# Five probability row buffers, held-back score products and a third transpose bank in a hybrid decoder trunk

## The chip, the cores and the metric

The kernel runs on one core of a Trainium2 chip. The metric is device time in microseconds of one execution; the profile's span is the time from the first to the last instruction of the program.

## The reference

The trunk has two layers over 1040 tokens (16 learned meta tokens in front of 1024) of width 1024, all in float32. Each layer is a pre-RMSNorm, a mixer, a multiplication by SiLU of a gate, an output projection and a residual addition. Layer 0 is multi-head latent attention with 8 heads; layer 1 is a gated linear recurrence (RG-LRU). A final RMSNorm follows.

```python
proj = h @ w_in                              # 384 | 256 | 64 | 1024
q_lat, kv_lat, k_rope, gate = jnp.split(proj, ...)
q  = rmsnorm(q_lat, q_norm_g) @ w_uq         # 8 heads x (128 + 64)
kv = rmsnorm(kv_lat, kv_norm_g) @ w_ukv      # 8 heads x (128 + 128)
...
s = (q_nope . k_nope + q_rope . k_rope) * scale
p = softmax(where(causal mask, s, -1e30))
attn = p @ v
y = attn * silu(gate);  h = h + y @ w_out
```

## The kernel before, in words

Every product is made of three single-pass products on the high and low parts of its operands (`mm3`). `hi_of` makes the high part on ACT (a copy with rounding), `lo_of` the low part on DVE (the difference). Nearly every tile therefore goes PSUM to ACT to DVE before TensorE can use it again.

PSUM has eight banks. The ring of a tag is its number of buffers: before attention, tag `t` (transposes, `ps_t`) has 2 and tag `m` (products, `ps_m`) has 6. In attention `t` has 2, `g` (projections and weighted sums) has 2, and `s2` (scores) has 2 buffers of two banks each.

*Start and latent stage.* The token tiles are taken in the order 8, 0, 1, ..., 7; tile 8 has 16 rows and is multiplied in a packed form (`mm_stack`). `x_tile` normalises a tile on ACT and DVE, transposes it on TensorE (`transpose_in`) and splits it. `lat_mm` makes the products `pq` and `pk` of a tile in two banks of `ps_m`; `lat_norm` normalises them, `lat_post` transposes them (`qt`, `kt`) and splits them. The row `g_a` is spread over all partitions with a product (`rb_ga`) and copied back by DVE. The stage of the rotary queries and gates (`rope_q_chunk`, `a_gate`) follows.

*Attention.* The 1040 rows are cut into 9 tiles of 116 rows (the last has 112). A unit is one head and one tile t; it uses the keys up to its own end, so its row is 116 (t + 1) columns long. `scores` makes the products in `s2` banks (the last tile's row needs both buffers), adds the mask and takes the extreme on DVE (line 501), writes exponentials to a row buffer `p` on ACT (line 509) and normalises the row (DVE for t < 6, ACT behind that). `transposes` turns the row in groups of three key blocks (`tr` = 0, 1, 2), each in one bank `pt`, and splits each into `pth` and `ptl`. `weighted` multiplies three tiles at a time with the values. The main loop runs over the 72 units:

```python
    for u, (h, t) in enumerate(units):
        if u + LEAD < len(units):
            scores(*units[u + LEAD])
        ...
        for f in fill[h, t]:
            f()
        transposes(h, t)
```

`fill` holds the K, Q and V projections of later chunks and heads (`k_unit`, `q_unit`, `v_unit`), and `LEAD` is 3. The row buffers `p` are three, each of 1040 columns.

*What sets the order.* The program text is not the issue order. A planner simulates the engines and puts on each one, among the instructions whose inputs and buffers it thinks ready, the one that was written first. On the chip each engine then keeps this order. `behind(marks, f, ...)` adds an order: what `f` issues on the engine of a mark comes behind that mark on that engine; it is an order of issue, with no wait for the mark's end.

Of the kernel before, what the change touches and what calls it, by code (L numbers as in the profile page):

```python
# [17 lines left out]
P = 128  # L18
# [26 lines left out]
GRP = 3  # L45
CH = [(g * GRP * QB, min(GRP * QB, T - g * GRP * QB)) for g in range((NQB + GRP - 1) // GRP)]
CHW = GRP * QB
MASKW = 8 * QB


def segments(e):
# [11 lines left out]
def trunk(ctx, tc, x, meta, a_norm_g, a_w_in, a_q_g, a_kv_g, a_w_uq, a_w_ukv, a_w_out,  # L63
# [12 lines left out]
    def bc(t):  # L76
        return t.bitcast(F32)

    def hi_of(dst, src):
        nc.scalar.activation(dst, src, AF.Copy)  # L80

    def lo_of(dst, src, hi):
        nc.vector.tensor_tensor(dst, src, bc(hi), ALU.subtract)  # L83

    def mm3(ps, lh, ll, rh, rl, start, stop, **kw):
        nc.tensor.matmul(ps, lh, rh, start=start, stop=False, **kw)  # L86
        nc.tensor.matmul(ps, lh, rl, start=False, stop=False, **kw)  # L87
        nc.tensor.matmul(ps, ll, rh, start=False, stop=stop, **kw)  # L88

    def mm_stack(ps, xp, k, n, wh, wl):  # L90
        if k:
# [16 lines left out]
    def ps_tag(tag, bufs):  # L108
        return lambda name: ps_pool[0].tile([P, 512], F32, name=name, tag=tag, bufs=bufs)

    ps_t, ps_g, ps_m = ps_tag("t", 2), ps_tag("g", 2), ps_tag("m", 6)
    def ps_2(name):
        return ps_pool[0].tile([P, 2, 512], F32, name=name, tag="s2", bufs=2)

# [11 lines left out]
    make_identity(nc, ident)  # L126

    def rms_r(ms, n, w, name):
        v = sml.tile([P, w], F32, name=f"v_{name}", tag="rv")[:n]
        r = sml.tile([P, w], F32, name=f"r_{name}", tag="rr")[:n]  # L130
        t = sml.tile([P, w], F32, name=f"t_{name}", tag="rt")[:n]
        root = nc.scalar.activation(t, ms, AF.Sqrt, bias=eps[:n])
        nc.vector.tensor_scalar(v, ms, -0.5, -0.5 * EPS, ALU.mult, ALU.add)
        nc.vector.reciprocal(t, t)
        if w == 1:
            nc.vector.scalar_tensor_tensor(r, t, v, t, ALU.mult, ALU.mult)
        else:
            nc.vector.tensor_tensor(r, t, t, ALU.mult)
            nc.vector.tensor_tensor(r, r, v, ALU.mult)
        nc.vector.scalar_tensor_tensor(r, r, 1.5, t, ALU.add, ALU.mult)  # L140
        return r, root
# [16 lines left out]
    def transpose_in(xn, n, t0, xth, xtl, name):  # L158
        for j in range(2):
            pt = ps_t(f"xt_{name}_{j}")  # L160
            pv = pt.rearrange("p (a b) -> p a b", b=P)[:, :, :n]
            for a in range(4):
                k = 4 * j + a
                nc.tensor.transpose(pv[:, a], xn[:n, k * P:(k + 1) * P], ident[:n, :n])
            hs = xth[:, 4 * j:4 * j + 4, t0:t0 + n]
            hi_of(hs, pv)
            lo_of(xtl[:, 4 * j:4 * j + 4, t0:t0 + n], pv, hs)

    def load_wcols(w, c0, nk, ncols, name):
        st = stage(name)  # L170
# [51 lines left out]
    def x_tile(i, xs):  # L222
        t0, n = TOK[i]
        j0 = t0 if n == P else 0
        junk = xth[:, :, j0:j0 + P]
        marks = normalise(xs[:n], xs[:n], n, g_a, junk, f"a{i}")
        if n < P:
            nc.gpsimd.memset(bc(xpk[:, :, n:STK]), 0.0)
            transpose_in(xs, n, 0, xpk, xpk[:, :, STK:], f"a{i}")
            nc.gpsimd.tensor_copy(xth[:, :, t0:t0 + n], bc(xpk[:, :, :n]))  # L230
            nc.gpsimd.tensor_copy(xtl[:, :, t0:t0 + n], bc(xpk[:, :, STK:]))
        else:
            transpose_in(xs, n, t0, xth, xtl, f"a{i}")
        return marks
# [26 lines left out]

    def lat_norm(i, pq, pk):
        t0, n = TOK[i]
        ms = sml.tile([P, 2], F32, name=f"lms{i}", tag="lms")[:n]
        lt = pa1.tile([P, QL + KVL], F32, name=f"lt{i}", tag="lt", bufs=2)[:n]
        nc.scalar.activation(lt[:, :QL], pq[:n, :QL], AF.Square, scale=float(QL ** -0.5), accum_out=ms[:, 0:1])
        nc.scalar.activation(lt[:, QL:], pk[:n, :KVL], AF.Square, scale=float(KVL ** -0.5), accum_out=ms[:, 1:2])
        kc = pa1.tile([P, 2, HR], F32, name=f"kc{i}", tag="kc", bufs=2)[:n]
        kn = pa1.tile([P, 2, HR], F32, name=f"kn{i}", tag="kn", bufs=2)[:n]
        kr = pa1.tile([P, 3, DR], F32R, name=f"kr{i}", tag="kr", bufs=1)[:n]  # L270
        krv = pk[:n, KVL:KVL + DR].rearrange("p (a b) -> p a b", a=2)
        nc.vector.tensor_tensor(kc, krv, csk[:n, i:i + 1, :HR].broadcast_to([n, 2, HR]), ALU.mult)
        nc.vector.tensor_tensor(kn, krv, csk[:n, i:i + 1, HR:].broadcast_to([n, 2, HR]), ALU.mult)
        r, _ = rms_r(ms, n, 2, f"lat{i}")
        nc.vector.scalar_tensor_tensor(lt[:, :QL], pq[:n, :QL], r[:, 0:1], g_q[:n, :QL], ALU.mult, ALU.mult)
        nc.vector.scalar_tensor_tensor(lt[:, QL:], pk[:n, :KVL], r[:, 1:2], g_q[:n, QL:], ALU.mult, ALU.mult)
        nc.vector.tensor_tensor(kc[:, 0], kc[:, 0], kn[:, 1], ALU.subtract)
        nc.vector.tensor_tensor(kc[:, 1], kn[:, 0], kc[:, 1], ALU.add)
        kf = kc.rearrange("p a b -> p (a b)")
        nc.vector.tensor_copy(kr[:, 0], kf)  # L280
        nc.vector.tensor_tensor(kr[:, 1], kf, bc(kr[:, 0]), ALU.subtract)
        nc.vector.tensor_copy(kr[:, 2], bc(kr[:, 0]))
        return lt, bc(kr.rearrange("p a b -> p (a b)"))
# [28 lines left out]
    n0 = TOK[order[0]][1]  # L312
    nc.sync.dma_start(g_a[:n0, :], a_norm_g[0:1, :].broadcast_to([n0, D]))
    xs0 = x_load(order[0])
    marks = x_tile(order[0], xs0)
    rbs = []
    for c in range(0, D, 512):
        ps = ps_m(f"rb_ga{c}")
        nc.tensor.matmul(ps, ones, g_a[0:1, c:c + 512], start=True, stop=True)
        rbs.append(ps)  # L320
    for c in range(0, D, 512):
        nc.vector.tensor_copy(g_a[:, c:c + 512], rbs[c // 512])
    for k in range(2):
        behind(marks, load_wlat, k)
    x_tile(order[1], x_load(order[1]))
    for k in range(2, KT):
        behind(marks, load_wlat, k)
    x_tile(order[2], x_load(order[2]))
# [60 lines left out]
    def a_gate(m):  # L389
        raw = load_wcols(a_w_in, LATW + m * P, KT, P, f"wg{m}")  # L390
        wh, wl = split_page(raw, [P, KT, P], f"wg{m}")
        for c, (c0, cw) in enumerate(CH):
            ps = ps_m(f"ga{m}_{c}")[:, :cw]
            for k in range(KT):
                mm3(ps, wh[:, k], wl[:, k], xth[:, k, c0:c0 + cw], xtl[:, k, c0:c0 + cw], k == 0, k == KT - 1)
            nc.scalar.activation(Y[:, m, c0:c0 + cw], ps, AF.Silu)

    for m in range(KT):
        a_gate(m)
        if m < 6:  # L400
            if m % 3 == 0:
                wr = rope_w(m // 3)
            rope_q_chunk(m // 3, m % 3, *wr)
# [2 lines left out]


    st_p1.close()
    st_p3, ps_pool[0] = open_pool("ps3", space=PSUM)
    st_at, pat = open_pool("at", bufs=2)  # L410
    maskt = pat.tile([QB, MASKW], F32, name="maskt", bufs=1)
# [1 line left out]
    nc.gpsimd.affine_select(out=maskt[:, MASKW - QB:], in_=maskt[:, MASKW - QB:], pattern=[[-1, QB]],  # L413
                            compare_op=ALU.is_ge, fill=-NEG, base=0, channel_multiplier=1)
    KV, QW, KK, QQ, VV, PP, PT = {}, {}, {}, {}, {}, {}, {}

    def load_pair(h):
        st = stage(f"wkv{h}")
# [9 lines left out]
    def k_unit(h, c):  # L428
# [4 lines left out]
        c0, cw = CH[c]  # L433
        ps = ps_g(f"pk{h}_{c}")[:, :cw]
        for k in range(VKT):
            mm3(ps, kvw[0][:, k, hh * 256:hh * 256 + DN], kvw[1][:, k, hh * 256:hh * 256 + DN],
                klh[:, k, c0:c0 + cw], kll[:, k, c0:c0 + cw], k == 0, k == VKT - 1)
        kh, kl = KK[h]
        hi_of(kh[:, c0:c0 + cw], ps)
        lo_of(kl[:, c0:c0 + cw], ps, kh[:, c0:c0 + cw])  # L440

    def q_unit(h, c):
        qw, hh = QW[h // 2], h % 2
# [27 lines left out]
    def scores(h, t):  # L471
# [7 lines left out]
        tiles = [segs[i:i + 2] for i in range(0, len(segs), 2)]  # L479
        m = sml.tile([QB, 2], F32, name=f"m{h}_{t}", tag="m")[:n]  # L480
        l = sml.tile([QB, 2], F32, name=f"l{h}_{t}", tag="l")[:n]
        p = pat.tile([QB, T], F32, name=f"p{h}_{t}", tag="p", bufs=3)[:n]
        pss = []
        a, b_, r_ = qh[:, off:off + n], ql[:, off:off + n], qr[:, off:off + n]
        for s, sg in enumerate(tiles):
# [10 lines left out]
            ns, k0 = len(sg), sg[0][0]  # L496
            pv = ps2[:n, :ns, :w]
            if s == len(tiles) - 1:
                lo = MASKW - QB - (ns * w - n)
                mk = maskt[:n, lo:lo + ns * w].rearrange("p (a b) -> p a b", a=ns)  # L500
                MKD[h, t] = nc.vector.tensor_tensor_reduce(pv, pv, mk, 1.0, -NEG, ALU.add, ALU.min, m[:, s:s + 1])  # L501
            else:
                nc.vector.tensor_reduce(m[:, s:s + 1], pv, AX.XY, ALU.min)
# [16 lines left out]
    def transposes(h, t):  # L520
# [8 lines left out]
        for tr in range(g + 1):  # L529
# [3 lines left out]
            pv = pt[:, :GRP * QB].rearrange("p (a b) -> p a b", b=QB)[:, :, :n]  # L533
            for j, kb in enumerate(kbs):
                k0, nk = QBLK[kb]
                nc.tensor.transpose(pv[:nk, j], p[:, k0:k0 + nk], ident[:n, :n])  # L536
            nfull = sum(1 for kb in kbs if QBLK[kb][1] == QB)
            parts = [(0, nfull, QB)] if nfull else []
            if nfull < len(kbs):
# [1 line left out]
            for j0, j1, nk in parts:  # L541
                dh = pth[:nk, j0:j1, off:off + n]
                hi_of(dh, pv[:nk, j0:j1])
                lo_of(ptl[:nk, j0:j1, off:off + n], pv[:nk, j0:j1], dh)

    def weighted(h, g):
        c0, cw = CH[g]
# [106 lines left out]
    for i, t in enumerate((5, 7, 8)):  # L654
        fill[H - 1, t].append(lambda i=i: a_out0(i, ps_g))
    load_pair(0)
    k_unit(0, 0)
    q_unit(0, 0)
    for u in range(-LEAD - 2, 0):
        for c in (1, 2):  # L660
            if 3 * c - LEAD - 2 == u:
                k_unit(0, c)
            if 3 * c - LEAD - 1 == u:
                q_unit(0, c)
# [2 lines left out]
    pending = None  # L667
    for u in range(LEAD):
        scores(*units[u])
    for u, (h, t) in enumerate(units):  # L670
        if u + LEAD < len(units):
            scores(*units[u + LEAD])
        if pending:
            weighted(*pending)
            pending = None
        for f in fill[h, t]:
            f()
        transposes(h, t)
        if t % 3 == 2:
            pending = (h, t // 3)  # L680
    weighted(*pending)
# [299 lines left out]
    def late(i, c, done):  # L981
        ms = sml.tile([P, 1], F32, name=f"msb{i}", tag="msb", bufs=2)
        square(i, c, ms)
        v = sml.tile([P, 1], F32, name=f"v_f{i}", tag="rv")
        r = sml.tile([P, 1], F32, name=f"r_f{i}", tag="rr")
        t = sml.tile([P, 1], F32, name=f"t_f{i}", tag="rt")
        nc.scalar.activation(t, ms, AF.Sqrt, bias=msa[i])
# [140 lines left out]
```

## Time and profile before

| | before |
|---|---|
| median of 3 runs | 913.55 us (913.08 to 913.59) |
| the profiled execution | 913.81 us |
| its span | 912.0 us |
| TensorE (PE) busy | 887.0 us, 97% |
| VectorE (DVE) busy | 584.5 us, 64% |
| ScalarE (ACT) busy | 469.0 us, 51% |
| GpSimd (POOL) busy | 44.5 us, 5% |

Busy time is the time in which an engine had at least one instruction in work. Successive products overlap, so that a busy PE need not be at its peak; idle time, on the other hand, is time without any product. A view of waits puts the idle time of an engine down to the instruction that ended it.

### The profile page before, as it was taken

How to read it: one execution, taken by the hardware profiler on the slowest of the kernel's cores; microseconds unless marked ns; L12 is line 12 of the kernel's file. 1: busy time of each engine (PE TensorE's matmuls, PEld its weight loads, DVE VectorE, ACT ScalarE, POOL GpSimd, SP SyncE). 2: the span in 40 equal slices, each digit the busy share in tenths (PEclk: the TensorE clock that was granted, in tenths of full speed). 3: DMA queues.
4: the chain of work that ended last, by engine and by line, in shares of the span. 5: the costliest groups of instructions: out<-in, count | busy, mean ns of one | idle time of the engine just before them, and what ended most of it. 6: DMA issues, size and time to landing. Idle time of an engine off the chain costs nothing.

```text
span 912.0 us, 13696 instructions
## 1 busy us (share of the span) xinstructions
PE 887.0 (97%) x5291; PEld 817.2 (90%) x5291; DVE 584.5 (64%) x1211; ACT 469.0 (51%) x941; POOL 44.5 (5%) x46
## 2 busy tenths in 40 slices
PE   7999999999999999999999999999999999999996
PEld 4989999998999999999998878799989989897885
DVE  6567434226676676776677457757393764868997
ACT  6554323215665656646656235634835457365455
POOL 3000000000000000000000000000020110212200
PEclk9999999999999999999999999999999999999999
DMA  7123254321010010010003435241111121237624
GB/s 261 62 59 92 61 135 127 87 72 57 16 56 18 14 58 16 17 63 16 17 24 116 152 99 179 78 81 47 47 47 49 45 57 37 95 91 230 140 69 184
DMA packets 71169, 72.25 MB, mean 79 GB/s; under 512 B 15056, under 2 KB 52688, under 8 KB 71104
## 3 DMA queue, kind: packets, MB, share of 16 engines
q1 hardware_dynamic: 68928, 67.19, 24.0%
q0 software_dynamic: 2176, 4.19, 2.7%
q8 instruction: 41, 0.67, 0.3%
q14 instruction: 24, 0.20, 0.1%
HBM read 58.65 MB, written 12.71 MB: 78 GB/s over the span
## 4 chain that ended last, share of the span: by engine, by line
PE 92%; ACT 3%; DVE 2%; issue 1%; DMA 1%; SPq 0%; ACTq 0%; DVEq 0%
PE pt L536 4%; PE pu L88 3%; PE ga L86 3%; PE pu L86 3%; PE ga L87 3%; PE ga L88 3%; PE pu L87 3%; PE ao L86 3%; PE ao L88 3%; PE ao L87 3%; PE pg L87 3%; PE pg L88 3%; PE pg L86 3%; PE s L491 2%; PE b L86 2%; PE b L88 2%
## 5 line engine op out<-in xcount | busy, mean ns | idle before, releaser
L509 ACT ACTIVATE p<-s,m 116x116 f32<-116x116 f32 (+4 forms) x80 | 55.4, 694 | 42.8 <-PE pt L536 15.2
L80 ACT ACTIVATE pth<-pt 116x348 fp32r<-116x348 f32 (+5 forms) x152 | 57.4, 397 | 28.6 <-PE pt L536 24.9
L83 DVE TENSOR_TENSOR ptl<-pt,pth 116x348 fp32r<-116x348 f32 (+5 forms) x152 | 63.9, 437 | 9.8 <-ACT pth L80 9.2
L88 PE MATMUL pu<-x2h,l_wu 128*128 128x348 f32 (+1 forms) x192 | 61.5, 321 | 0.4 <-DVE l_wu L83 0.4
L86 PE MATMUL ga<-xth,h_wg 128*128 128x348 f32 (+1 forms) x192 | 61.7, 322 | 0.0
L88 PE MATMUL ga<-xth,l_wg 128*128 128x348 f32 (+1 forms) x192 | 61.7, 321 | 0.0
L86 PE MATMUL pu<-x2h,h_wu 128*128 128x348 f32 (+1 forms) x192 | 61.7, 322 | 0.0
L87 PE MATMUL pu<-x2l,h_wu 128*128 128x348 f32 (+1 forms) x192 | 61.7, 321 | 0.0
L87 PE MATMUL ga<-xtl,h_wg 128*128 128x348 f32 (+1 forms) x192 | 61.6, 321 | 0.0
L501 DVE CUSTOM_DVE_ANT_0 s<-s,maskt 116x116 f32<-116x116 f32 (+8 forms) x72 | 49.4, 686 | 17.6 <-PE s L495 17.6
L536 PE MATMUL pt<-ident,p 116*116 116x116 f32 (+1 forms) x360 | 54.2, 262 | 0.9 <-DVE ptl L83 0.4
L87 PE MATMUL pg<-x2l,h_wbg 128*128 128x512 f32 x128 | 50.6, 395 | 0.0
L86 PE MATMUL ao<-wah,yh_a 128*128 128x512 f32 x128 | 50.5, 396 | 0.0
L88 PE MATMUL pg<-x2h,l_wbg 128*128 128x512 f32 x128 | 50.3, 393 | 0.0
L86 PE MATMUL pg<-x2h,h_wbg 128*128 128x512 f32 x128 | 50.2, 392 | 0.0
L88 PE MATMUL ao<-wah,yl_a 128*128 128x512 f32 x128 | 50.1, 393 | 0.0
L87 PE MATMUL ao<-wal,yh_a 128*128 128x512 f32 x128 | 49.8, 390 | 0.0
L491 PE MATMUL s<-kh,qh 128*116 128x348 f32 (+7 forms) x120 | 42.1, 351 | 6.7 <-ACT p L509 6.7
L536 PEld LDWEIGHTS pt<-ident,p 116*116 116x116 f32 (+1 forms) x360 | 41.5, 135 | 4.1 <-PE pt L536 1.6
L87 PE MATMUL o<-ptl,v 116*128 116x348 f32 (+1 forms) x144 | 45.1, 313 | 0.0
L88 PE MATMUL o<-pth,v 116*128 116x348 f32 (+1 forms) x144 | 43.9, 305 | 0.0
L86 PE MATMUL o<-pth,v 116*128 116x348 f32 (+1 forms) x144 | 43.0, 299 | 0.6 <-ACT pth L80 0.6
(328 smaller groups left out, 2654.9 us busy)
## 6 DMA issues: line engine op xcount, KB each, us to landing
wg<-in_a_w_in SPq DMA_DIRECT2D x8, 512.0 KB, 4.1
wa<-in_a_w_out SPq DMA_DIRECT2D x8, 512.0 KB, 3.5
wu<-in_b_w_in SPq DMA_DIRECT2D x8, 512.0 KB, 4.0
wbg<-in_b_w_in SPq DMA_DIRECT2D x8, 512.0 KB, 3.9
hr<-hscr SPq DMA_DIRECT2D x8, 512.0 KB, 6.9
out_h<-hr SPq DMA_DIRECT2D x16, 256.0 KB, 2.1
x<-in_x SPq DMA_DIRECT2D x7, 512.0 KB, 3.8
wq<-in_b_w_out SPq DMA_DIRECT2D x6, 512.0 KB, 3.5
```

Of the source, the lines that this page charges most:

```text
L80: nc.scalar.activation(dst, src, AF.Copy)
L83: nc.vector.tensor_tensor(dst, src, bc(hi), ALU.subtract)
L86: nc.tensor.matmul(ps, lh, rh, start=start, stop=False, **kw)
L87: nc.tensor.matmul(ps, lh, rl, start=False, stop=False, **kw)
L88: nc.tensor.matmul(ps, ll, rh, start=False, stop=stop, **kw)
L491: nc.tensor.matmul(ps, a, kth[:, k0:k0 + w], start=True, stop=False)
L501: MKD[h, t] = nc.vector.tensor_tensor_reduce(pv, pv, mk, 1.0, -NEG, ALU.add, ALU.min, m[:, s:s + 1])
L509: MK[h, t] = nc.scalar.activation(dst, pv, AF.Exp, bias=mx, scale=-1.0, accum_out=l[:, s:s + 1])
L536: nc.tensor.transpose(pv[:nk, j], p[:, k0:k0 + nk], ident[:n, :n])
```

## The change

It has six parts. (1) The row buffers `p` become five slots of the sizes that their tiles need; `PSLOT` gives the slot of each tile. (2) In the main loop `scores` of unit u+3 is issued on PE behind the second (or only) transposition group of unit u-1. (3) The mask table is five blocks wide in place of eight; its segments are read as overlapping windows (`mask_of`). (4) Before attention tag `t` gets three banks and tag `m` five. (5) At the start, the `g_a` copies and the next tile's work on ACT and DVE are issued behind the split of the 16-row tile. (6) On entry into attention a one-element exponential is issued behind the last SiLU, and the second K unit goes ahead of the first Q unit. Rings of small statistics tiles get two buffers in place of four.

```diff
-MASKW = 8 * QB
+MASKW = 5 * QB
+PSLOT = (0, 1, 2, 3, 4, 1, 2, 3, 4)
...
     def hi_of(dst, src):
-        nc.scalar.activation(dst, src, AF.Copy)
+        return nc.scalar.activation(dst, src, AF.Copy)
...
-    ps_t, ps_g, ps_m = ps_tag("t", 2), ps_tag("g", 2), ps_tag("m", 6)
+    nt = [3]
+
+    def ps_t(name):
+        return ps_tag("t", nt[0])(name)
+
+    def ps_m(name):
+        return ps_tag("m", 8 - nt[0])(name)
+
+    ps_g = ps_tag("g", 2)
...
-        v = sml.tile([P, w], F32, name=f"v_{name}", tag="rv")[:n]
+        v = sml.tile([P, w], F32, name=f"v_{name}", tag="rv", bufs=2)[:n]
...
             hs = xth[:, 4 * j:4 * j + 4, t0:t0 + n]
-            hi_of(hs, pv)
-            lo_of(xtl[:, 4 * j:4 * j + 4, t0:t0 + n], pv, hs)
+            marks = [hi_of(hs, pv), lo_of(xtl[:, 4 * j:4 * j + 4, t0:t0 + n], pv, hs)]
+        return marks
...
-            transpose_in(xs, n, 0, xpk, xpk[:, :, STK:], f"a{i}")
+            marks = (*transpose_in(xs, n, 0, xpk, xpk[:, :, STK:], f"a{i}"), *marks)
...
-        ms = sml.tile([P, 2], F32, name=f"lms{i}", tag="lms")[:n]
+        ms = sml.tile([P, 2], F32, name=f"lms{i}", tag="lms", bufs=2)[:n]
...
-    marks = x_tile(order[0], xs0)
+    split0 = x_tile(order[0], xs0)
+    marks = split0[2:]
+    split0 = split0[:2]
...
-        nc.vector.tensor_copy(g_a[:, c:c + 512], rbs[c // 512])
+        behind(split0, nc.vector.tensor_copy, g_a[:, c:c + 512], rbs[c // 512])
...
-    x_tile(order[1], x_load(order[1]))
+    behind(split0, x_tile, order[1], x_load(order[1]))
...
-            nc.scalar.activation(Y[:, m, c0:c0 + cw], ps, AF.Silu)
+            silu = nc.scalar.activation(Y[:, m, c0:c0 + cw], ps, AF.Silu)
+        return silu
 
     for m in range(KT):
-        a_gate(m)
+        silu = a_gate(m)
...
     st_p1.close()
+    nt[0] = 2
     st_p3, ps_pool[0] = open_pool("ps3", space=PSUM)
...
+    def mask_of(n, ns, w):
+        m = maskt[:n, MASKW - QB - (w - n) - (ns - 1) * n:]
+        return bass.AP(m.tensor, m.offset, [m.ap[0], (n, ns), (1, w)])
...
-        p = pat.tile([QB, T], F32, name=f"p{h}_{t}", tag="p", bufs=3)[:n]
+        sl = PSLOT[t]
+        pw = max(QBLK[u][0] + QBLK[u][1] for u in range(NQB) if PSLOT[u] == sl)
+        p = pat.tile([QB, pw], F32, name=f"p{h}_{t}", tag=f"p{sl}", bufs=1)[:n]
...
-                lo = MASKW - QB - (ns * w - n)
-                mk = maskt[:n, lo:lo + ns * w].rearrange("p (a b) -> p a b", a=ns)
+                mk = mask_of(n, ns, w)
...
-                nc.tensor.transpose(pv[:nk, j], p[:, k0:k0 + nk], ident[:n, :n])
+                tp = nc.tensor.transpose(pv[:nk, j], p[:, k0:k0 + nk], ident[:n, :n])
+            if tr < 2:
+                last = tp
...
     load_pair(0)
+    behind([silu], nc.scalar.activation, warm, ones[:, 0:1], AF.Exp)
     k_unit(0, 0)
-    q_unit(0, 0)
+    ku = k_unit(0, 1)
+    behind([ku], q_unit, 0, 0)
     for u in range(-LEAD - 2, 0):
         for c in (1, 2):
-            if 3 * c - LEAD - 2 == u:
+            if 3 * c - LEAD - 2 == u and c > 1:
                 k_unit(0, c)
...
+    last = None
     for u, (h, t) in enumerate(units):
         if u + LEAD < len(units):
-            scores(*units[u + LEAD])
+            behind([last] if last else [], scores, *units[u + LEAD])
...
-        transposes(h, t)
+        last = transposes(h, t)
...
-        v = sml.tile([P, 1], F32, name=f"v_f{i}", tag="rv")
+        v = sml.tile([P, 1], F32, name=f"v_f{i}", tag="rv", bufs=2)
```

## Rows read from the trace of the kernel before

**Rows 1.** The page: span; busy time of PE and its weight loads.
```profile
span 912.0 us, 13696 instructions
...
PE 887.0 (97%) x5291; PEld 817.2 (90%) x5291; DVE 584.5 (64%) x1211; ACT 469.0 (51%) x941; POOL 44.5 (5%) x46
```

**Rows 2.** Windows: stretch, its length, each engine's busy time, granted clock, DMA share, GB/s.
```profile
0.00:17.00 17.00, 10.18 (x38) 5.45 (x39) 10.05 (x21) 10.25 (x18) 5.52 (x12) 1.00 0.81 276
17.00:60.00 43.00, 41.22 (x271) 39.05 (x269) 26.57 (x102) 23.84 (x68) 2.47 (x1) 1.00 0.21 74
...
204.00:215.00 11.00, 9.61 (x63) 8.94 (x62) 4.23 (x12) 5.37 (x12) 0.00 (x0) 1.00 0.29 84
215.00:512.00 297.00, 289.78 (x1979) 276.28 (x1978) 208.95 (x558) 175.35 (x429) 0.20 (x1) 1.00 0.12 37
512.00:888.00 376.00, 375.50 (x1944) 329.82 (x1944) 255.05 (x309) 195.60 (x275) 35.13 (x31) 1.00 0.32 91
```

**Rows 3.** Timeline, PE's first products: start, length, engine, instruction, [idle before].
```profile
3.20 3.75 PE L319 MATMUL rb_ga<-g_a,ones 1*128 1x512 f32 x4 [3.20 <-DMA g_a<-in_a_norm_g]
```

**Rows 4.** Waits of PE, 215 to 512 us: in total, times, longest.
```profile
PE s L491 <- ACT p L509: 5.7, 8, 1.0
```

**Rows 5.** Waits of ACT, 212 to 515 us.
```profile
ACT p L509 <- PE pt L536: 15.2, 13, 2.4
...
ACT p L509 <- issue: 11.4, 6, 2.7
```

**Rows 6.** Timeline in attention, PE and ACT.
```profile
262.82 0.44 PE L491 MATMUL s<-kh,qh 128*116 128x464 f32 x1
...
265.93 0.29 PE L536 MATMUL pt<-ident,p 116*116 116x116 f32 x1
...
266.30 0.94 ACT L509 ACTIVATE p<-s,m 116x812 f32<-116x812 f32 x1 [2.70 <-issue]
...
270.98 0.41 PE L491 MATMUL s<-kh,qh 128*112 128x344 f32 x1 [0.92 <-ACT p L509]
```

**Rows 7.** Instructions of the tile `pt`: shortest, median, longest in ns.
```profile
L80 ACT ACTIVATE pth<-pt x152: 257/452/472, 216.8 to 511.2; 116x348 fp32r<-116x348 f32 x72, 116x116 fp32r<-116x116 f32 x24, 116x232 fp32r<-116x232 f32 x24, 116x336 fp32r<-116x336 f32 x16
```

**Rows 8.** Timeline of the start.
```profile
7.03 1.00 PE L164 MATMUL xt_a<-ident,x 16*128 16x16 f32 x8
7.61 1.27 DVE L322 COPY g_a<-rb_ga 128x512 f32<-128x512 f32 x2
9.35 1.06 ACT L153 ACTIVATE xth<-x 128x1024 fp32r<-128x1024 f32 x1 [2.57 <-DMA x<-in_x]
10.40 0.32 ACT L80 ACTIVATE kll<-xt_a 128x64 fp32r<-128x64 f32 x2
10.92 0.55 PE L93 MATMUL pq<-wlh,kll 128*48 128x384 f32 x1 [2.89 <-DVE kll L83]
...
14.47 0.33 PE L93 MATMUL pq<-wlh,kll 128*48 128x384 f32 x1
...
14.99 1.28 DVE L156 SCALAR_TENSOR_TENSOR x<-x,r_a,g_a 128x1024 f32<-128x1024 f32 x1
```

**Rows 9.** Timeline of the latent stage.
```profile
45.36 0.61 DVE L275 SCALAR_TENSOR_TENSOR lt<-pq,r_lat,g_q 128x384 f32<-128x384 f32 x1
...
47.65 0.29 ACT L294 ACTIVATE ks<-qt 128x128 fp32r<-128x128 f32 x1
...
47.99 1.19 PE L164 MATMUL xt_a<-ident,x 128*128 128x128 f32 x8 [1.37 <-ACT ks L294]
```

**Rows 10.** Timeline of the entry into attention.
```profile
207.65 0.51 DVE L83 TENSOR_TENSOR kl<-pk,kh 128x348 fp32r<-128x348 f32 x1
...
207.78 0.42 PE L88 MATMUL pqn<-qlh,l_wq 128*128 128x348 f32 x1 [0.41 <-DVE l_wq L83]
...
212.49 1.28 ACT L509 ACT_TABLE_LOAD   x1
...
214.28 0.41 PE L491 MATMUL s<-kh,qh 128*116 128x348 f32 x1 [0.98 <-ACT p L509]
```

More of the change, by code (lines that the diff above doesn't have):

```diff
@@ L79, in hi_of @@
     def hi_of(dst, src):
-        nc.scalar.activation(dst, src, AF.Copy)
+        return nc.scalar.activation(dst, src, AF.Copy)
     def lo_of(dst, src, hi):
-        nc.vector.tensor_tensor(dst, src, bc(hi), ALU.subtract)
+        return nc.vector.tensor_tensor(dst, src, bc(hi), ALU.subtract)
     def mm3(ps, lh, ll, rh, rl, start, stop, **kw):
@@ L87, in mm3 @@
         nc.tensor.matmul(ps, lh, rl, start=False, stop=False, **kw)
-        nc.tensor.matmul(ps, ll, rh, start=False, stop=stop, **kw)
+        return nc.tensor.matmul(ps, ll, rh, start=False, stop=stop, **kw)
     def mm_stack(ps, xp, k, n, wh, wl):
@@ L435, in k_unit @@
         for k in range(VKT):
-            mm3(ps, kvw[0][:, k, hh * 256:hh * 256 + DN], kvw[1][:, k, hh * 256:hh * 256 + DN],
-                klh[:, k, c0:c0 + cw], kll[:, k, c0:c0 + cw], k == 0, k == VKT - 1)
+            last = mm3(ps, kvw[0][:, k, hh * 256:hh * 256 + DN], kvw[1][:, k, hh * 256:hh * 256 + DN],
+                       klh[:, k, c0:c0 + cw], kll[:, k, c0:c0 + cw], k == 0, k == VKT - 1)
         kh, kl = KK[h]
@@ L440, in k_unit @@
         lo_of(kl[:, c0:c0 + cw], ps, kh[:, c0:c0 + cw])
+        return last
     def q_unit(h, c):
@@ L544, in transposes @@
                 lo_of(ptl[:nk, j0:j1, off:off + n], pv[:nk, j0:j1], dh)
+        return last
     def weighted(h, g):
```

## Prediction

> **What bounds the kernel now.** The page comes first: TensorE is busy for 887.0 us of the span of 912.0, in 5291 products [rows 1]. The change removes no product of TensorE, so only its idle time can be won, 25.0 us in all. The windows say where that time lies [rows 2]: the span minus PE's busy time is 6.8 us in the first 17, 1.8 us up to 60, 1.4 us from 204 to 215, 7.2 us from 215 to 512 (attention), and 0.5 us from 512 to 888. From 60 to 204 there is none, so the rest of the 25.0, 7.3 us, lies in the last 24. The change touches neither that end nor the first 3.2 us, which wait for a load [rows 3]. What stays in reach is 3.6 + 1.8 + 1.4 + 7.2 = 14.0 us, or 1.5%. And what is won early is kept: behind attention TensorE has 0.5 us of idle time in 376, so no other engine or load is near to taking the gain back.
>
> In attention PE's list of waits names one cause: score products wait 8 times, 5.7 us, for exponentials on ACT [rows 4]. A score product waits because its score bank (there are two) has not been read. So the question is what ACT was doing. Its own list [rows 5] shows the exponential idle for 15.2 us (13 times) until a transposition `pt` on PE ended, and 11.4 us (6 times) under "issue", where the view names nobody. The timeline shows both to be one thing [rows 6]: a single transposition runs at 265.93 to 266.22, and at 266.30 the exponential of the next 812 columns starts after 2.70 us of idling. The exponential writes a `p` row, of which there are three buffers, and it waits for the transpositions that read the row of three tiles before. It ends late, the chain moves on by one bank, and at 270.98 PE idles 0.92 us for an exponential. This last row comes three times, 72 us (two heads) apart.
>
> **Attention: the row buffers.** Five slots in place of three, and by the table the tile that last used a slot lies at least four back (1 and 5, 2 and 6, and so on; five or more across heads). The exponential at 266.30 would no longer wait for the transposition at 265.93, and its 2.70 us of idle time goes; so would most of the 26.6 us in [rows 5]. PE gains only what it idles itself. Of its 7.2 us there, 5.7 are listed under the exponential. I take 5.0: nearly all of the 5.7, and nothing of the rest. The upper end is 7.2. The mask table shrinks from 928 to 580 columns and is read with shifted, overlapping rows; the same elements pass through DVE, so I count nothing, since DVE is busy for only 209 of 297 us there [rows 2].
>
> **Attention: score products held back.** The scores of tile u+3 are now issued behind the first two transposition groups of tile u-1. No engine gets an instruction more; an order on PE's queue is added. It costs nothing if those transpositions can run anyway: their row was normalised some tiles ago. But they need one of two transposition banks, and one is free only when ACT and DVE have copied it out, 0.45 us for the ACT half alone [rows 7]. If PE stands there, the scores stand behind it, then the masking on DVE, then the exponential. In the stretch that I read, the scores of the eighth tile ran at 262.82, three us ahead of the transposition at 265.93, the second group of the fourth tile, behind which they would now stand [rows 6]. So the hold does bite. The cover is the other PE work that may pass (K, Q, V units, weighted sums). I count zero; without cover, 0.45 us for the units with three groups, 3 in each of 8 heads: 10.8 us. That end makes this part 5.0 - 10.8 = -5.8.
>
> **Start.** The first packed products wait until 10.92, 2.89 us idle, for DVE's split of the small tile [rows 8]. Its transposes end at 8.03, but ACT's half, 0.32 us for two, stands behind the square of the next tile, which waits for its load until 9.35. The change puts both halves of the split ahead of that square and ahead of the two `g_a` copies (1.27 us together, from 7.61): the split would end by about 8.8 and the copies by 10.1, before the next tile's square ends at 10.41, so the delayed copies are hidden. No load moves: the request for the next tile is issued outside the held block. Yet the 2 us are not all gained. What PE does next, the transposes of the full tile, waits for its normalising multiplication on DVE (14.99 to 16.27), and the packed products before it wait for weight splits on the same two engines. This chain shortens only by what the split took out of the queue after 9.35, about 0.3 us, which I take. Bounds: up to 1.3 if eight more packed products, half of 0.33 us apart, fit in ahead of it; down to -1.7 because of the clock. The products of 384 columns at 10.92 take 0.55 us and at 14.47 0.33 us: the pace of 1.2 GHz and then that of 2.4 GHz, though the granted clock column says 1.00 throughout. An earlier start with pauses could put as long a stretch at the lower pace, 10.92 to 14.47, behind 16.27, where PE hardly pauses any more; half of it would be lost.
>
> **Latent stage.** At 47.99 PE idles 1.37 us until ACT has copied the last piece of an old transposition bank, 47.65 to 47.94 [rows 9]. With three banks the next transposes need not wait for that one. Their second half still needs a bank, and the copies after them share ACT's queue, so I take 1.2 of the 1.8 us idle in this window; ends 1.8 and 0. The price is one bank less for the products, five in place of six. A tile then needs a bank of two tiles before; that was read at 45.36 to 45.97, two us before the next tile's transposes at 47.99 even start. I count nothing and keep -0.5 as the lower end. Smaller rings for the tiny statistics tiles (two in place of four) cost nothing: a buffer's last reader is two tiles back, on engines that keep their order.
>
> **Entry into attention.** Two things. The exponential's table load, 1.28 us on ACT at 212.49, holds the first exponential, and PE idles 0.98 us at 214.28 [rows 10]; the load now goes behind the last SiLU, some 5 us earlier. And the second K unit goes ahead of the first Q unit, which idled 0.41 us for its weights at 207.78. Against it: the first K bank, emptied by DVE at 207.65 to 208.16, is what the Q unit needs now, and the load (1.28) may land ahead of ACT's half of that very copy. So of 1.4 us I take 0.7; the ends are 1.4, and -1.3 if the load's 1.28 is paid at the Q unit and nothing comes back. The Trainium skill (ScalarE: Activation LUTs, What ACT_TABLE_LOAD costs) gives a switch a drain of 1.38 us on top of 1.28, 2.66 in all; by that, as an estimate, this term would be up to 1.4 larger, the sum 8.6 and the time 904.9. The rows show no room for that drain: the score product that waits for the first exponential starts at 214.28, 0.51 us behind the load's end at 213.77.
>
> **Sum.** 5.0 + 0.3 + 1.2 + 0.7 = 7.2 us. The profiled execution took 913.81, so 906.6; the median of before is 0.26 lower (913.55), and 906.3 is the forecast. On the level of the median, all upper ends, 7.2 + 1.3 + 1.8 + 1.4 = 11.7, give 901.9; all lower ends, -5.8 - 1.7 - 0.5 - 1.3 = -9.3, give 922.9.
>
> **Rivals.** (1) The buffers are not the limit; the two score banks are. Then exponentials start earlier but PE's order still reaches each score bank too soon, at the end of a head above all, where the last tile takes both banks. For it: even with rows free a bank turns only after mask and exponential; against it: the long idle times before exponentials are not on the mask's side. Attention gains 0.5: 2.7 us in all, 910.9. The Trainium skill (Trace Analysis, Optimization Strategy) says that a gap that keeps repeating on the busy engine can mean too little SBUF or PSUM for the next tile; the trace agrees with the repeating, and leaves open which memory. (2) Slower: the hold on the scores becomes the wait, as priced above, 10.8 us: 7.2 - 10.8 = -3.6, or 917.2. It decides from 7.2 / 24 = 0.3 us per three-group tile. For it: the two banks and the scores seen between groups; against it: PE waits for a transposition bank only in small pieces now. (3) No change: attention's waits move to other places and the small terms cancel, 913.5.
>
> **Chances.** Forecast 0.63, rival 1 0.14, rival 2 0.13, rival 3 0.10. Faster by over 0.2% (1.8 us, about what a measurement can tell from no change) gets the first two less 0.01, 0.76; within it 0.11; slower 0.13. The forecast's own range is 901.9 to 910. For 8 in 10 the range takes in rival 1 and rival 3, and some beyond the sum of upper ends because an idle time ends with a pipeline to refill: 900.5 to 914.5.
>
> **What would show it.** Attention right: the exponential's waits for `pt` and for "issue" nearly gone, score products' wait under 1.5 us, PE idle in that stretch near 2 us. Rival 1: the score products' 5.7 us stay while ACT's waits go. Rival 2: transpositions waiting for `pth` or `ptl` copies. Start: first packed product near 9, full tile's transposes near 16.1. Latent: no wait for the copy of line 294. Entry: a table load near 207 and no wait at the first exponentials. Wrong would make it an order of PE's products that differs much from this one: the issue order is made by a planner that I read only through its result, and a new bubble of 0.3 us per tile outweighs all.

## The result: 0.7% slower

The changed kernel takes 920.43 us (median of 5 runs, 919.95 to 921.59) against 913.55 us (912.84 to 913.60) in the same session: a ratio of 1.0074, 95% interval 1.0063 to 1.0084, or 6.9 us slower where I had forecast 7.2 us faster. It lies beyond my range, and beyond the 917.2 us of the rival that was to end on this side.

The page of the profile after, its span and its busy time of TensorE, and the windows to be held against [rows 2]:

```profile
span 918.7 us, 13620 instructions
...
PE 891.1 (97%) x5291; PEld 818.8 (89%) x5291; DVE 582.6 (63%) x1211; ACT 470.0 (51%) x942; POOL 43.4 (5%) x46
```

```profile
0.00:17.00 17.00, 12.22 (x45) 6.08 (x46) 10.93 (x21) 10.93 (x19) 5.78 (x12) 1.00 0.82 276
17.00:60.00 43.00, 42.50 (x282) 41.35 (x281) 27.65 (x111) 24.47 (x71) 1.46 (x1) 1.00 0.26 87
...
204.00:215.00 11.00, 9.35 (x66) 8.88 (x65) 6.15 (x19) 5.94 (x16) 0.00 (x0) 1.00 0.30 85
215.00:512.00 297.00, 286.06 (x1930) 271.93 (x1929) 202.72 (x542) 173.19 (x419) 0.20 (x1) 0.99 0.12 36
```

The same 5291 products, 4.1 us more busy time, and a span 6.6 us longer (912.04 to 918.67). The first two windows gained (PE busy 12.22 for 10.18 and 42.50 for 41.22), the entry lost a little, and attention lost: 286.06 us of 297 for 289.78.

Windows cut at fixed times mix different work, so below I cut by work. Each number is a difference of two starts or ends in the trace:

| stage | before | after | difference |
|---|---|---|---|
| to the first gate product (start and latent stage) | 87.76 | 85.29 | -2.47 |
| gate products, first to last | 118.20 | 117.93 | -0.27 |
| entry: last gate product to attention's first transposition | 9.93 | 10.52 | +0.59 |
| attention: first transposition to last `o` product | 298.13 | 306.46 | +8.33 |
| of it heads 0 to 6 (to the seventh head's last write of `Y`) | 257.0 | 256.8 | -0.2 |
| of it the last head | 41.1 | 49.7 | +8.5 |
| last `o` product to the end | 398.03 | 398.47 | +0.44 |

The loss is the last head alone. At the end of the seventh head the changed kernel is still 2.3 us ahead (470.53 for 472.87).

**The lists of waits.** PE from 215 to 512 us after, against [rows 4], and ACT in the same window, against [rows 5] (waited for; us in total, times, longest):

```profile
PE o L87 <- ACT pth L81: 5.2, 5, 1.6
PE pqn L87 <- DVE kl L84: 2.6, 3, 0.9
PE o L88 <- DVE ptl L84: 1.6, 1, 1.6
```

```profile
ACT p L529 <- DVE m L521: 41.3, 38, 4.1
ACT pth L81 <- PE pt L556: 40.8, 48, 4.1
```

The change did to these lists what I said. The exponential waits neither for `pt` nor under "issue" any more, almost only for the row minimum `m` of its own scores (0.8 us, in three times, are put down to the reciprocal `l` of a row's sum), and no score product waits for an exponential. But PE's idle time has only gone to other names: weighted sums `o` now wait for the copies `pth` and `ptl` of a transposed row, and a Q unit waits for a K bank (`kl`).

**Heads 0 to 6: one wait for another.** The timeline of the changed kernel shows the two new idle times; both come three times, 72 us apart, as the old one did:

```profile
280.74 0.40 PE L87 MATMUL o<-pth,v 116*128 116x344 f32 x1 [0.70 <-ACT pth L81]
...
293.83 0.42 PE L87 MATMUL pqn<-qlh,h_wq 128*128 128x344 f32 x1 [0.86 <-DVE kl L84]
```

3 x (0.70 + 0.86) = 4.7 us. In the kernel before it was 0.92 us at 270.98 [rows 6], with a second of 0.50 before the score products at 283.54, also three times: 3 x 1.42 = 4.3 us.

**The last head: a block of weight splits, and nothing to put over it.** The output weights come in four parts; ACT makes the high half of each (`wah`) and DVE the low half (`wal`). These splits are marked, in both kernels, behind exponentials of the last head: two behind that of the fifth tile and two behind that of the sixth (4, 4, 5, 5 in the code, which counts from 0). First the kernel before, ACT and then PE:

```profile
475.63 2.00 ACT L80 ACTIVATE wah<-wa 128x1024 fp32r<-128x1024 f32 x2
477.53 0.62 ACT L80 ACTIVATE yh_a<-Y 128x512 fp32r<-128x512 f32 x1
478.05 0.83 ACT L509 ACTIVATE p<-s,m 116x696 f32<-116x696 f32 x1
478.86 0.46 ACT L80 ACTIVATE pth<-pt 116x348 fp32r<-116x348 f32 x1
479.20 2.01 ACT L80 ACTIVATE wah<-wa 128x1024 fp32r<-128x1024 f32 x2
```

```profile
479.02 0.47 PE L491 MATMUL s<-kh,qh 128*116 128x464 f32 x1 [0.96 <-ACT p L509]
479.32 0.37 PE L492 MATMUL s<-kl,qh 128*116 128x464 f32 x1
479.53 0.38 PE L493 MATMUL s<-kh,ql 128*116 128x464 f32 x1
```

Then the changed kernel, ACT, DVE and PE:

```profile
472.81 0.84 ACT L529 ACTIVATE p<-s,m 116x696 f32<-116x696 f32 x1 [2.09 <-DVE m L521]
...
473.98 3.90 ACT L81 ACTIVATE wah<-wa 128x1024 fp32r<-128x1024 f32 x4
477.77 0.46 ACT L81 ACTIVATE pth<-pt 116x348 fp32r<-116x348 f32 x1
```

```profile
475.07 2.36 DVE L595 TENSOR_TENSOR wal<-wa,wah 128x1024 fp32r<-128x1024 f32 x2
...
478.27 2.35 DVE L595 TENSOR_TENSOR wal<-wa,wah 128x1024 fp32r<-128x1024 f32 x2
480.54 0.51 DVE L84 TENSOR_TENSOR ptl<-pt,pth 116x348 fp32r<-116x348 f32 x1
```

```profile
472.72 0.76 PE L556 MATMUL pt<-ident,p 116*116 116x116 f32 x6
...
478.27 0.42 PE L87 MATMUL o<-pth,v 116*128 116x348 f32 x1 [1.52 <-ACT pth L81]
...
481.11 0.66 PE L88 MATMUL o<-ptl,v 116*128 116x348 f32 x1 [1.58 <-DVE ptl L84]
...
483.01 0.42 PE L556 MATMUL pt<-ident,p 116*116 116x116 f32 x1
483.10 0.72 PE L512 MATMUL s<-kh,qh 128*116 128x464 f32 x1
483.62 0.59 PE L513 MATMUL s<-kl,qh 128*116 128x464 f32 x1
484.00 0.59 PE L514 MATMUL s<-kh,ql 128*116 128x464 f32 x1
...
497.68 0.43 PE L87 MATMUL o<-pth,v 116*128 116x348 f32 x1 [1.59 <-ACT pth L81]
...
514.29 0.81 PE L556 MATMUL pt<-ident,p 112*116 112x112 f32 x6 [1.31 <-DVE ptl L84]
```

Before, the exponential of the sixth tile (696 columns) waited for a row and fell between the two pairs of splits, with the `pth` copy behind it. With a row of its own it goes first, at 472.81, and all four splits follow in one block, 3.90 us on ACT, with 2.36 and 2.35 us on DVE. Two groups transposed at 472.72 wait behind the block for their copies, so both transposition banks are full. The next transposition runs at 483.01; until it has, the scores of the eighth tile (464 columns, ten products) may not start, and they start at 483.10, four us later than before, although the changed kernel came 2.3 us early into this head. PE stands idle for 1.52 and 1.58 us in between, and for 1.59 and 1.31 us later in the head; with the splits spread (run 3 below) none of these four is left, and the longest idle time of the last head is 0.7 us.

### The profile page after: what moved, and what is told of

The parts are those of the page before. It is cut to its first block, busy times and chain, and to the rows that moved or that the text cites. A ratio compares the mean times of both kernels' runs of the same rounds, so it can differ in the third digit from the quotient of the medians.

```text
span 918.7 us, 13620 instructions
## 1 busy us (share of the span) xinstructions
PE 891.1 (97%) x5291; PEld 818.8 (89%) x5291; DVE 582.6 (63%) x1211; ACT 470.0 (51%) x942; POOL 43.4 (5%) x46
## 4 chain that ended last, share of the span: by engine, by line
PE 89%; DVE 4%; ACT 4%; issue 1%; DMA 1%; SPq 0%; ACTq 0%; DVEq 0%
PE pu L89 3%; PE pu L87 3%; PE pu L88 3%; PE pt L556 3%; PE ga L87 3%; PE ga L88 3%; PE ga L89 3%; PE ao L89 3%; PE ao L87 3%; PE ao L88 3%; PE pg L88 3%; PE pg L89 3%; PE pg L87 3%; PE b L87 2%; PE b L88 2%; PE b L89 2%
## 5 line engine op out<-in xcount | busy, mean ns | idle before, releaser
L81 ACT ACTIVATE pth<-pt 116x348 fp32r<-116x348 f32 (+5 forms) x152 | 58.0, 398 | 45.2 <-PE pt L556 43.4
L556 PE MATMUL pt<-ident,p 116*116 116x116 f32 (+1 forms) x360 | 56.4, 263 | 1.9 <-DVE ptl L84 1.8
L87 PE MATMUL o<-pth,v 116*128 116x348 f32 (+1 forms) x144 | 44.5, 309 | 5.5 <-ACT pth L81 5.5
L89 PE MATMUL o<-pth,v 116*128 116x348 f32 (+1 forms) x144 | 44.4, 308 | 0.0
L81 ACT ACTIVATE yh_a<-Y 128x512 fp32r<-128x512 f32 x32 | 20.2, 630 | 41.5 <-PE ao L88 38.8
```

Of the source, the lines that this page charges most:

```text
L81: return nc.scalar.activation(dst, src, AF.Copy)
L89: return nc.tensor.matmul(ps, ll, rh, start=False, stop=stop, **kw)
L556: tp = nc.tensor.transpose(pv[:nk, j], p[:, k0:k0 + nk], ident[:n, :n])
```

## The experiments

"Attention" is the stage of the table above; its times come from one trace of each kernel. Times of the kernel before beside these runs: 913.82, 914.09 and 913.69 us (first to third set of four).

**1. The hold taken away.**
```diff
-            behind([last] if last else [], scores, *units[u + LEAD])
+            scores(*units[u + LEAD])
```


> The changed kernel without the hold: score products are issued freely, the five row buffers stay. Theory A (in the last head the four output-weight splits, marked behind the exponentials of tiles 4 and 5, now stand in one block on ACT and DVE because these exponentials no longer wait for row buffers): the block stays, so the time stays near the changed kernel's, 918 to 922 us. Theory B (the hold itself makes PE wait): 912 us or less.

Measured: 915.52 us, ratio 1.0016 (1.0007 to 1.0026); attention 300.5, last head 41.3 (six more of its score products than in the changed kernel start before the seventh head's end here). The block theory alone is wrong: here the block is there, and attention is 6.0 us shorter all the same, because score products run under it:

```profile
476.40 0.44 PE L512 MATMUL s<-kh,qh 128*116 128x406 f32 x1 [0.38 <-ACT qh L470]
...
480.34 0.37 PE L516 MATMUL s<-ks,qr 128*116 128x464 f32 x1
```
```profile
476.23 3.90 ACT L81 ACTIVATE wah<-wa 128x1024 fp32r<-128x1024 f32 x4
```

These two rows of PE are the first and the last of twenty score products, of the seventh and eighth tile; the ten of the eighth are those that the changed kernel holds until 483.10. The hold theory alone is not borne out either: it expected 912 or less. New theory: the loss takes both, the block and the hold.

**2. Three rows again, hold kept.**
```diff
-        p = pat.tile([QB, pw], F32, name=f"p{h}_{t}", tag=f"p{sl}", bufs=1)[:n]
+        p = pat.tile([QB, T], F32, name=f"p{h}_{t}", tag="p", bufs=3)[:n]
```


> The changed kernel with three row buffers of 1040 columns as before, the hold kept. Theory A: the exponentials wait for rows again, tile 5's above all, the block of weight splits falls into two pairs and the last head gives back its 8 us or so: 911 to 914 us. Theory B: the hold stays and with it the loss, 918 us or more.

Measured: 916.83 us, 1.0032 (1.0020 to 1.0044), between the two; attention 302.0, last head 43.6. With three rows the splits stand in two pairs again, and the last head still loses 2.4 us to the hold: PE is idle for 1.30 us before a weighted sum at 479.48, where the kernel before ran score products, and for 1.31 us at 509.14. Heads 0 to 6 lose 1.5 us (258.5).

**3. The splits spread, all else kept.**
```diff
-    for kk, t in enumerate((3, 3, 3, 3)):
-        ... behind([MK[H - 1, (4, 4, 5, 5)[kk]]], part_out, kk)
+    for kk, t in enumerate((3, 3, 3, 4)):
+        ... behind([MK[H - 1, (4, 5, 6, 7)[kk]]], part_out, kk)
```


> The changed kernel with the four weight splits marked behind the exponentials of tiles 4, 5, 6 and 7 in place of 4, 4, 5, 5, nothing else. Theory A: the block of 3.9 us on ACT is cut into 2.0 + 1.0 + 1.0, PE's waits for the copies of tiles 2 and 3 of the last head and the slow stretch behind them go: 912 to 915 us. Theory B: no change, 919 to 921 us.

Measured: 912.45 us, 0.9986 (0.9977 to 0.9995); attention 297.9, last head 41.1, as theory A expected. (`MK` holds the exponentials.) Against the changed kernel (920.43) eight us come back from the place of the splits, hold and rows as they were.

**4. Neither rows nor hold.** Edits 1 and 2 together.

> The changed kernel without the hold and with three row buffers as before; what stays are the parts of start, latent stage and entry (and the narrower mask). Both theories: the changed kernel led by 2.2 us at the first transposition of attention, and attention is then that of before: 911 us (910 to 912).

Measured: 914.82 us, 1.0013 (1.0004 to 1.0022). A miss of both theories: the first gate product comes at 85.12, the gain of the early stages is there, but entry and attention take 0.6 and 1.4 us more than before, and what follows attention 0.8 us more than in runs 1 to 3, 0.6 of it idle time before an output product at 513.74.

**5. No hold in the last head only.**
```diff
-            behind([last] if last else [], scores, *units[u + LEAD])
+            behind([last] if last and h < H - 1 else [], scores, *units[u + LEAD])
```


> The changed kernel, its block of weight splits kept, but the scores are held only in heads 0 to 6. Theory 'both are needed' (the block of splits empties the transposition banks late, and the hold takes away the score products that could cover this): the last head (from the seventh head's last write of Y to the last output product) falls from 49.7 to about 41.2 us, heads 0 to 6 stay at 256.8, and the time falls to 911.5 to 913. Theory 'the block alone': the last head stays near 49 us and the time at 919 to 921. Theory 'the hold costs a little in every head': the last head gains no more than 4 us, time about 916 to 917.

Measured: 913.94 us, 0.9996 (0.9987 to 1.0005); attention 299.2, last head 41.3. The block stays and 7.3 us go: "both are needed" holds for nearly all of the loss. In the last head the block alone costs 0.1 us (41.3 for 41.1), the hold alone 2.4 (run 2), the two together 8.5. The time is 1 us above what the theory expected, and attention 1.3 above run 3: unheld, score products of the last head run ahead of the seventh's end (565 have started by then, for 559), which ends 1.2 us later, and the last head doesn't get shorter by as much.

**6 to 8. The entry**, on top of edit 3: the early exponential left out (6), the first Q unit ahead of the second K unit again (7), both (8).
```diff
-    behind([silu], nc.scalar.activation, warm, ones[:, 0:1], AF.Exp)      # 6 and 8
-    ku = k_unit(0, 1)                                                     # 7 and 8
-    behind([ku], q_unit, 0, 0)
+    q_unit(0, 0)
-            if 3 * c - LEAD - 2 == u and c > 1:
+            if 3 * c - LEAD - 2 == u:
```


> The weight splits spread (marks 4, 5, 6, 7, the last of them called one tile later), and the early exponential behind the last SiLU left out, so that the table load stands again at the first exponential. Theory 'the load is in the way' (ACT loads the table for 1.28 us ahead of its half of the first K bank's copy, and the first Q unit idles 1.7 us for that bank): the wait of the first Q unit goes, but the first exponential waits for its table again; entry (last gate product to first transposition) 9.5 to 10.5 us against 10.52, time 911.5 to 912.5. Theory 'the order of the K units is in the way': the Q unit still idles 1 us or more, and the entry gets about 1 us longer, 11 to 11.5 us.

> The weight splits spread as before, the early exponential kept, but the first Q unit ahead of the second K unit, as in the kernel before. Theory 'the load is in the way': the Q unit takes the other bank of the two, and the wait for the bank moves to the second K unit, no shorter than 1 us; entry 10.3 to 11 us, time 912 to 913. Theory 'the order of the K units is in the way': the wait of 1.7 us goes, the entry falls to 9.0 to 9.5 us, time about 911.2.

> The weight splits spread and both edits of the entry undone (late table load, Q unit first): the rest of the change is kept. The entry should take again the 9.93 us of the kernel before, 0.6 less than in the changed kernel, and the time should be 911.5 to 912.3. If the two edits are worth something together after all, it is over 912.5.

Measured: 912.11, 911.57 and 911.71 us; ratios 0.9980 (0.9971 to 0.9989), 0.9968 (0.9956 to 0.9981), 0.9972 (0.9961 to 0.9983). Their intervals overlap, so the trace has to tell them apart: the entry takes 9.64, 9.54 and 9.92 us; both edits in, as in the changed kernel, 10.52. Each edit alone gains 0.3 to 0.4 us on 9.93, and the two together lose 0.6. The rows of the changed kernel show how:

```profile
203.90 0.44 ACT L408 ACTIVATE Y<-ga 128x344 f32<-128x344 f32 x1
204.34 1.28 ACT L318 ACT_TABLE_LOAD   x1
205.64 0.20 ACT L318 ACTIVATE warm<-ones 1x1 f32<-1x1 f32 x1
205.75 0.78 ACT L81 ACTIVATE kh<-pk 128x348 fp32r<-128x348 f32 x2
```
```profile
206.79 0.43 PE L87 MATMUL pqn<-qlh,h_wq 128*128 128x348 f32 x1 [1.66 <-DVE kl L84]
```

Two K units fill both banks, the load stands ahead of the copy that empties the first, and the Q unit waits 1.66 us. With the late load (6) that wait is 0.3; with Q first (7) the second bank is free for the Q unit, and what is left are two waits of 0.4. Run 6 came as the theory of the load expected and run 7 close to that of the order, so neither edit is to blame alone; run 8 came as expected.

**9. No hold, 10. three rows**, both with edit 3 and Q first (as run 7).

> Weight splits spread and the first Q unit ahead of the second K unit, the five row buffers kept, and no hold on the scores anywhere. Attention is read from its first transposition to its last output product: 298.1 us in the kernel before, 297.6 with spread splits, Q first and hold. Theory 'the rows were the limit and the hold eats the gain': without the hold attention falls to 294 to 296 us, time 908.5 to 910.5. Theory 'the two score banks are the limit once the rows are not': attention stays at 297 to 299 us, the score products' waits for exponentials do not go to zero (1.6 us in the changed kernel without hold), time 911 to 913.

> Weight splits spread, Q first, the hold kept, but three row buffers of full width as in the kernel before. Theory 'the five rows are worth something under the hold': attention is 1.5 us or more above the 297.6 of the same kernel with five rows, about 299 to 300.5 us, time 913 to 914.5. Theory 'rows and hold trade one wait for another': attention 297 to 298.5 us, time 911.3 to 912.5.

Measured: 913.86 us, 1.0009 (1.0000 to 1.0018), attention 299.7, for 9, worse than either theory expected; 912.46 us, 0.9985 (0.9976 to 0.9994), attention 298.0, for 10, as its second theory expected. Run 7, with hold and five rows, has 297.7. So once the splits are spread the hold is no cost in this stage but a gain of 2.0 us beside five rows, and five rows are worth 0.3 us beside three. Behind attention runs 9 and 10 both take 0.8 us more than run 7 (399.3 for 398.5), with the idle time of 0.6 us before an output product that run 4 has too. By whole times run 9 is slower than run 7 (the intervals of their ratios are apart), and run 10 can't be told from it. Without the hold one wait of the old kind is still there (run 9, PE, 215 to 512 us):

```profile
PE s L512 <- ACT p L529: 1.8, 3, 0.6
```

And with three rows under the hold (run 10, same window) there are no waits for exponentials either, but these:

```profile
PE o L87 <- ACT pth L81: 2.6, 5, 0.6
PE pt L556 <- DVE ptl L84: 1.8, 7, 0.3
```

**11. The start alone, 12. the latent stage alone**, each as an edit of the kernel before.

> The kernel before with only the edits of the start (both halves of the small tile's split ahead of the copies of the gain and of the next tile's square). My term for it was 0.3 us (bounds -1.7 to 1.3). If the 2.5 us that the changed kernel is ahead at its first gate product come mostly from the start, this kernel's first gate product comes at 85.8 to 86.6 (before: 87.76) and the time is 911.8 to 912.8. If my term was right, it comes at 87.3 to 87.7 and the time is 913.2 to 913.8.

> The kernel before with only three transpose banks and five product banks in the latent stage (and the smaller statistics ring). My term was 1.2 us (bounds -0.5 to 1.8): the wait of 1.37 us for the copy of the old bank goes, the first gate product comes at 86.4 to 86.8 (before: 87.76), time 912.2 to 912.8. If the wait only moves to the next bank or the products, the first gate product stays at 87.5 or later and the time at 913.3 or more.

Measured: for 11, 914.01 us, 1.0000 (0.9991 to 1.0009), first gate product at 86.79, 0.97 ahead of before (0.2 of it because PE's first load came that much sooner), between the two expectations, with a time above both. For 12, 911.65 us, 0.9977 (0.9968 to 0.9986), first gate product at 85.73, 2.03 ahead, better than expected. The changed kernel and runs 1 to 10 have one early stage among them, and its first gate product comes at 85.12 to 86.50, so one such reading is good to some 0.7 us; for run 12 the measured ratio, 2.1 us, says the same as the trace. There PE is never idle from 17 to 60 us:

```profile
17.00:60.00 43.00, 43.00 (x288) 41.71 (x287) 28.38 (x113) 24.40 (x71) 2.44 (x1) 1.00 0.27 87
```

**Attention in the kernels that change it:**

| rows | hold | weight splits | attention, us |
|---|---|---|---|
| 3 | no | two pairs (before) | 298.1 |
| 3 | no | two pairs (run 4) | 299.5 |
| 5 | yes | block (changed kernel) | 306.5 |
| 5 | no | block (run 1) | 300.5 |
| 5 | not in the last head | block (run 5) | 299.2 |
| 3 | yes | two pairs (run 2) | 302.0 |
| 5 | yes | spread (runs 3, 6, 7, 8) | 297.9, 298.1, 297.7, 297.7 |
| 5 | no | spread (run 9) | 299.7 |
| 3 | yes | spread (run 10) | 298.0 |

The fastest version is run 7, 0.3% faster than before; the latent stage's third bank alone (run 12) gives 0.2%, so it is probably the larger part of that.

## Why the prediction was wrong

**The step that failed** is the hold: "The cover is the other PE work that may pass (K, Q, V units, weighted sums). I count zero". Up to the seventh head this is so (256.8 us for 257.0). In the last head the K, Q and V units end at 472.9, and the weighted sums wait for the same copies as the transpositions; the output products need the very splits that block ACT and DVE; the only cover left is the score products, which the hold forbids. I did have the lower end "without cover", but as 0.45 us for every three-group tile. It is nothing in seven heads and 8.5 us in one, because what was late was not one copy of 0.45 us but a block of 3.90. That block was a second thing I did not price: I followed the freed exponential to the score products, and not to what the planner had placed behind it on ACT's queue. The weight splits were in the diff's surroundings, not in the diff. Runs 1, 3 and 5 each remove one of the two conditions and get 6 to 9 us of attention back, and run 2, which puts the two pairs back with the rows, gets 6.1 us of the last head's 8.5 back; so this is shown.

**The price of the late block** divides in two. PE's recorded idle time in attention grows from 7.2 to 12.6 us, 5.4 of the 8.3; the products there last the other 2.9. Nearly all of that is one stretch at half pace. The ten score products from 483.10 on start 0.39 us apart, against 0.21 before for the same 464 columns, and take 4.00 us for 2.20; the eight weighted sums ahead of them, from 481.11, take 1.90 us for the 0.93 that the same eight take before, from 484.14. That is 2.8 us more. The granted clock says the same, last but two of this row:

```profile
483.00:488.00 5.00, 5.00 (x16) 4.08 (x16) 2.15 (x4) 1.05 (x3) 0.00 (x0) 0.54 0.35 129
```

From 481 to 487 it is 0.50, the lower level, 1.2 GHz; in the last of the five us it rises again.

**Row buffers, 5.0 us (upper end 7.2): mis-sized.** The mechanism was right, the exponential's waits went. The gain did not come: 0.3 us of attention by runs 7 and 10, or 1.1 us with the 0.8 behind it. The narrower mask costs nothing, as I counted: DVE takes 1.13 us for 928 masked columns in both kernels. The Trainium skill (Perfetto Trace Analysis, Optimization Strategy) reads a repeating gap on the busy engine as a possible want of buffers for the next tile; in this trace the gap repeated, five rows filled it, and gaps of 0.70 and 0.86 us repeated in other places. That the gap went elsewhere in heads 0 to 6 is my third rival, "attention's waits move to other places". The first, two score banks as the limit, has some of it: 1.8 us of waits for exponentials stay in run 9.

**The second rival's sign** was to be transpositions waiting for `pth` or `ptl`. The waits for these two copies came, 7.3 us up to 512 and 1.3 at 514.29, but mostly on the weighted sums, which stand ahead of the held scores; the transpositions have 0.5 and the 1.3 of it. The kind was right, the carrier and the price (10.8 us spread over 24 tiles) were not.

**Start, 0.3 us:** the first packed product came at 8.12 ("near 9") and the full tile's transposes at 15.97 ("near 16.1"). The clock, my lower end, took nothing here: products start at full pace from 13.14 on, before from 14.15. Alone the start is about 0.8 us at the first gate product, within my bounds; the measured ratio of run 11 doesn't tell it from nothing. **Latent stage, 1.2 us (upper end 1.8):** under-sized. The wait for the copy of line 294 is gone, no price for the missing product bank shows, and 2.03 us come back: I had counted one wait of the window where the third bank removed all its idle time, and a little more.

**Entry, +0.7 us:** -0.6, the wrong sign but within my ends. The lower end named it: the load "may land ahead of ACT's half of that very copy". The Trainium skill's price of a table switch (ScalarE: Activation LUTs, What ACT_TABLE_LOAD costs), a drain of 1.38 us on top of the load, is again not in the rows: the SiLU ends and the load starts at 204.34, and the next activation starts at 205.64, 0.02 behind the load's end.

**What stays open.** From the first to the last `b` product near the end the changed kernel takes 78.12 us for 77.70, with the same order of products and no wait of PE to show for it. It comes with the latent edit (run 12: 78.16, run 11: 77.70) though that edit touches nothing there; I did not find the cause. Run 4's attention is 1.4 us longer than before, 1.1 of it in the first head (44.5 us for 43.4), where PE has idle times of 0.79 and 0.25 us that the kernel before has not. Runs 2 and 10, which have three rows and differ ahead of the last head only in the order of the first Q and second K unit, also part early, 76.9 and 75.7 us for the first two heads. So the order on entry seems to cost about 1 us more inside attention when there are three rows; how is not shown. Nor did I find why five rows without the hold cost 1.6 us (run 9), of which PE's listed waits show less than they did before. A transposition's end is modelled at 0.26 us while the next can start 0.1 later, so waits of up to 0.16 us behind one don't show as idle time; that this is where the time goes was only argued.

## What to carry to other kernels

When a change frees an engine's instruction from a wait, list what its queue then brings next, above all work that is placed by a mark behind that instruction: a split harmless in two halves became a block of four, and cost 8.5 us under a hold that left nothing to run over it. Before holding work back to order it better, ask for each stretch, the last one too, what is left to run there if the hold's own condition is late. And two edits that each give a third of a microsecond can cost twice that together where they meet at one pair of banks; so measure them singly.

## What the hardware showed beyond that

In the changed kernel PE stood idle for 1.52 us before 478.27 and for 1.58 us before 481.11, with three products in between; from 477 to 481 it was busy for 1.16 us of 4. The granted clock was 1.00 up to 480, 0.87 in the next us, 0.50 from 481 to 487, while PE worked without a pause, and 1.00 again from 488. A single idle time of 1.59 us in the same kernel, before 497.68, was followed by products at full pace (granted clock 1.00 from 498 to 505), and so was one of 0.96 us before 479.02 in the kernel before. So in this case the price of the two waits grew by 2.8 us that no list of waits shows.
